# The low half of every fifth weight tile, made by an adding transfer

## The chip, the cores and the metric

The kernel runs on one core of a Trainium2 chip. The metric is device time in microseconds of that core for one execution; before the change the median of three runs is 1138.33 us (1137.66 to 1138.64). PE is the matrix engine, DVE the vector engine, ACT the scalar engine, POOL the general-purpose engine, and SP the engine that issues most transfers.

## The reference

A trunk of two layers works on 512 tokens of width 1024 in float32. Cut to what matters:

```python
for l in range(2):
    mod = silu(c) @ w_ada[l] + b_ada[l]            # shift, scale, gate
    u = rms_norm(x) * (1 + scale) + shift
    z = u @ w_in[l]                                # 18 column groups: q, k, v, gates, indexer, merge gates
    ya = sparse_attention(top 128 keys by the indexer's score)
    yb = sliding_window_attention(window 128, grouped heads, sinks)
    yc = stick_breaking_attention()
    merged = sum(sigmoid(m_b) * ((y_b * silu(gate_b)) @ w_br_b[l]))
    x = x + gate * (merged @ w_out[l])
return rms_norm(x) * final_g
```

Most of the arithmetic is the products with `w_in`, `w_br` and `w_out`, 1024 or 512 deep, over all 512 tokens.

## The kernel before

The matrix engine takes operands in a shortened 32-bit type (fp32r). To keep float32 accuracy, each operand is split into a high half, the operand rounded to that type, and a low half, the operand less its high half. A product then takes three matmuls: high by high, high weight by low activation, low weight by high activation. In the program's names `uh` and `ul` are the halves of the normalised activations, `whi` and `wlo` those of a weight tile.

Weights come in chunks of 128 x 512 (a few of 128 x 384 and 128 x 364). The class `Chunks` (from line 733) holds the sequence of all of them in the order of use, and does three things for chunk number i. `load` issues its transfer from HBM into a `wstage` tile, on SP's queue. `do_split` makes the halves: a cast of `wstage` to `whi`, on ACT, DVE or POOL, and a subtraction `wstage - whi` to `wlo`, on DVE or POOL. `get` hands the two to the matmuls. The split of a chunk stands up to three chunks ahead of its use; `wstage`, `whi` and `wlo` have four buffers each, so a chunk's halves can be written once the chunk four places earlier is used up. Some chunks, those of the conditioning product `w_ada`, are used raw, unsplit, by DVE. They count in the numbering.

A phase with the column groups `FIRST` (chunks of 512 and 384 columns, from `w_first`) opens each layer. The value phase follows (`w_v`, 364 columns a chunk; here the weight streams and the activation stands). Then come many streams woven together: the tiles of `w_t`, three mixers, the branch products (`w_br`), the conditioning product of the next layer. The output product (`w_o`) closes the layer.

The order of the instructions on each engine isn't that of the code. Every operation is recorded (class `Recorder`), with the engines that could do it, and `forward` lays all of them out by list scheduling: at each step the operation that can start first goes to its engine, by the prices in `price` and by priorities that `latest` works out from the round before. `order` does five rounds and keeps the one that ends first in the planner's own reckoning. So the order on every engine depends on what the planner assumes a transfer takes. `emit` then issues everything in that order, which is why nearly all instructions of the profile carry the line of `emit`, 621. In `price` a transfer that POOL issues holds POOL for 1.0; its `lag`, the bytes over a rate, and the lines in `forward` that the diff touches say when its data is there.

`both(out, a, b, op)` records a two-input operation for POOL or DVE. `cast(out, x, scale)` records a copy with rounding: without a scale for ACT, DVE or POOL, with a scale for ACT (`activation` with `Copy`) or DVE (`tensor_scalar`).

Of the kernel before, what the change touches and what calls it, by code (L numbers as in the profile page):

```python
# [29 lines left out]
OP = mybir.AluOpType  # L30
# [251 lines left out]
class Recorder:  # L282
# [149 lines left out]
    def forward(self):  # L432
        E = {e: {"free": 0.0, "port": 0.0, "mode": None, "ready": {}, "pend": []} for e in self.real}
        dma_free, lanes = 0.0, []
# [12 lines left out]
        def offer(x):  # L447
            if x.left == 0 and x.bound == 0:
                for e in x.alts:
                    heapq.heappush(E[e]["pend"], (max(x.est, x.soft.get(e, 0.0)), x.i))  # L450

        def give(c):
            while c.given < len(c.tiles) and c.free:
                t = c.tiles[c.given]
                c.given += 1
                if not t.users:
                    continue
                at, slot = heapq.heappop(c.free)
                t.slot, t.before, c.held[slot] = slot, c.held.get(slot), t
                for x in waiting[id(t)]:  # L460
                    x.est = max(x.est, at)
                    x.bound -= 1
                    offer(x)
# [7 lines left out]
        while len(out) < len(self.list):  # L471
            best = None
            for name, e in E.items():
                free, port, pend, ready = e["free"], e["port"], e["pend"], e["ready"]
                while pend and pend[0][0] <= free + 1e-9:
                    i = heapq.heappop(pend)[1]
                    ready[i] = self.list[i]
                mine = None
                for i in list(ready):
                    x = ready[i]  # L480
                    if x.taken:
                        del ready[i]
                        continue
                    y = x.alts[name]
                    at = max(free, port) if y.port else free
                    if len(x.alts) > 1 and self.elsewhere(x, name, at, E):
                        continue
                    key = (at, x.prio, i)
                    if mine is None or key < mine:
                        mine = key  # L490
                if mine is None or mine[0] > free + 1e-9:
                    while pend and self.list[pend[0][1]].taken:
                        heapq.heappop(pend)
                    if pend:
                        est, i = pend[0]
                        x = self.list[i]
                        at = max(est, port) if x.alts[name].port else est
                        key = (at, x.prio, i)
                        if (mine is None or key < mine) and not (len(x.alts) > 1 and self.elsewhere(x, name, at, E)):
                            mine = key  # L500
                        elif mine is None:
                            mine = None
                if mine is not None:
                    asked = max(free, self.list[mine[2]].est, self.list[mine[2]].soft.get(name, 0.0))
                    if best is None or (mine[0], asked, mine) < best[:3]:
                        best = (mine[0], asked, mine, name)
            assert best is not None, "no instruction may go"
            (at, _, i), name = best[2:]
            e, x = E[name], self.list[i]
            y = x.alts[name]  # L510
            x.taken, x.engine = True, name
            e["ready"].pop(i, None)
            hold = y.cost
            if name == "PE":
                if e["mode"] is not None and y.mode != e["mode"]:
                    hold += self.ENTER[y.mode]
                e["mode"] = y.mode
            x.start, x.hold = at, hold
            e["free"] = at + hold
            if y.port:  # L520
                E["POOL"]["port"] = at + y.lag + self.CROSS if name == "DVE" else at + hold
                E["DVE"]["port"] = at + y.lag - self.TOPORT
            if y.mode == "dma":
                if not x.writes:
                    x.end = at + 2.1
                else:
                    x.end = dma_free = max(at + (2.1 if at < 20.0 else 2.2 if y.lag < 0.22 else 3.0), dma_free) + y.lag * (1.2 if dma_free < 5.5 else 1.0)
                lanes.append(x.end)
                if name == "SP" and len(lanes) >= self.LANES:
                    e["free"] = max(e["free"], lanes[-self.LANES])  # L530
            else:
                x.end = at + y.lag + (hold - y.cost)
            out.append(x)
            for s in x.succs:
                s.est = max(s.est, x.end + self.between(x, s))
                s.left -= 1
                offer(s)
            for s in x.apart:
                for o in s.alts:
                    if o != name:  # L540
                        s.soft[o] = max(s.soft.get(o, 0.0), x.end + self.NEXT)
                s.left -= 1
                offer(s)
            for t in x.tiles:
                t.users -= 1
                t.done = max(t.done, x.end + self.CROSS)
                if t.users == 0:
                    heapq.heappush(t.pool.free, (t.done, t.slot))
                    give(t.pool)
# [99 lines left out]
def trunk(ctx, tc, xT, vecs, w_ss, w_gt, w_first, w_t, w_v, w_br, w_o, rope, consts, out):  # L649
# [8 lines left out]
    PE, ACT, DVE, POOL, SP = (rec.engine(e) for e in ("PE", "ACT", "DVE", "POOL", "SP"))  # L658
# [23 lines left out]
    f = lambda ap: ap.bitcast(F32)  # L682


    def in_psum(*views):
        return any(v.tile.pool.name[:3] == "ps_" for v in views)

    def cast(out, x, scale=None):
        if scale is None:
            ways = {"ACT": ("copy", (out, x), {}), "DVE": ("tensor_copy", (), dict(out=out, in_=x))}  # L690
            if not in_psum(x):
                ways["POOL"] = ("tensor_copy", (), dict(out=out, in_=x))
        else:
            ways = {"ACT": ("activation", (out, x, AF.Copy), dict(scale=scale)), "DVE": ("tensor_scalar", (out, x, scale, None), dict(op0=OP.mult))}
        rec.add(ways)

    def both(out, a, b, op_):
        how = ("tensor_tensor", (), dict(out=out, in0=a, in1=b, op=op_))
        rec.add({"DVE": how} if in_psum(a, b) else {"POOL": how, "DVE": how})
# [28 lines left out]
    class Chunks:  # L728
# [20 lines left out]
        def do_split(self, upto):  # L749
            while self.nsplit < min(upto + 1, len(self.seq)):  # L750
                i = self.nsplit
                if i >= self.nload:
                    break
                if not self.seq[i][1]:
                    t, n = self.raw.pop(i)
                    h = rec.tile("whi", [P, S], F32R)
                    lo = rec.tile("wlo", [P, S], F32R)
                    cast(h[:, :n], t[:, :n])
                    both(lo[:, :n], t[:, :n], f(h[:, :n]), OP.subtract)
                    self.split[i] = (h, lo)  # L760
                    self.used.add(i)
                self.nsplit += 1
# [1053 lines left out]
```

## Time and profile before

| what | value |
|---|---|
| median of three runs | 1138.33 us |
| the profiled execution, its own time | 1136.31 us |
| its span, first to last instruction | 1134.2 us |
| PE busy | 1116.3 us, 98% |
| DVE busy | 900.4 us, 79% |
| ACT busy | 615.8 us, 54% |
| POOL busy | 254.0 us, 22% |
| subtractions to `wlo` | 315 on DVE, 57 on POOL |
| moved by transfers | 159.86 MB, mean 141 GB/s |

The profile is one execution. Its span stands 2.1 us below the execution's own time. A matmul's row is longer than the distance to the next one, since matmuls are pipelined: PE's pace is read from the starts, its starvation from the list of waits.

### The profile page before, as it was taken

The numbers are of one execution on the slowest core, as the hardware profiler recorded it, in microseconds if no ns is written. First come the engines' busy times: TensorE is split into PE (matmuls) and PEld (weight loads), VectorE is DVE, ScalarE is ACT, GpSimd is POOL, SyncE is SP. The second block draws the span as 40 slices with busy tenths as digits, with TensorE's granted clock in tenths as the row PEclk, the third lists the DMA queues.
The fourth block names the chain that finished last, engine by engine and source line by source line (L and its number), as shares of the span: only waits on it lengthen the run. The fifth ranks groups of instructions, "written<-read, shape, count | busy, mean of one in ns | idle before, by whom it ended". The sixth has DMA issues, their size and how long they took to land.

```text
span 1134.2 us, 17655 instructions
## 1 busy us (share of the span) xinstructions
PE 1116.3 (98%) x5579; PEld 926.8 (82%) x5579; DVE 900.4 (79%) x1966; ACT 615.8 (54%) x1298; POOL 254.0 (22%) x340
## 2 busy tenths in 40 slices
PE   8999999999999999999999999999999999999997
PEld 6899877788878787788898988777888878877886
DVE  7865999999989896677475479999998898666544
ACT  6644765863556563444365357757436466444343
POOL 1110344632113220010011004555421222101101
PEclk9999999999999999999999999999999999999999
DMA  9644334354465566455634342253545445524342
GB/s 341 240 123 129 94 94 127 107 146 152 125 170 154 160 199 179 134 151 177 183 111 111 101 137 84 76 157 105 156 131 145 143 140 149 150 83 148 94 130 102
DMA packets 94301, 159.86 MB, mean 141 GB/s; under 512 B 14592, under 2 KB 29184, under 8 KB 94208
## 3 DMA queue, kind: packets, MB, share of 16 engines
q1 hardware_dynamic: 86096, 146.25, 43.7%
q10 hardware_dynamic: 8112, 12.49, 3.9%
q8 instruction: 44, 0.72, 0.3%
q14 instruction: 49, 0.40, 0.1%
HBM read 125.39 MB, written 4.19 MB: 114 GB/s over the span
## 4 chain that ended last, share of the span: by engine, by line
PE 87%; DVE 4%; DMA 3%; POOL 2%; ACT 1%; issue 1%; SPq 1%; DVEq 0%; POOLq 0%; ACTq 0%
PE ps_z L621 68%; PE ps_s L621 15%; PE ps_s L619 3%; SPq L621 1%; PE ps_z L619 1%; DVE X L621 1%; DMA Y<-in_w_ss 1%; DVE wlo L621 1%; POOL wlo L621 1%; DMA m<-zs 1%; DMA U<-X 1%; POOL Q L621 1%; DMA wstage<-in_w_br_c 0%; DVE m L621 0%; DVE t L621 0%
## 5 line engine op out<-in xcount | busy, mean ns | idle before, releaser
L621 PE MATMUL ps_z<-uh,whi 128*128 128x512 f32 (+1 forms) x905 | 353.9, 392 | 2.1 <-ACT KH L621 1.9
L621 PE MATMUL ps_z<-ul,whi 128*128 128x512 f32 (+1 forms) x905 | 351.5, 389 | 0.0
L621 PE MATMUL ps_z<-uh,wlo 128*128 128x512 f32 (+1 forms) x905 | 351.1, 388 | 0.0
L621 DVE TENSOR_TENSOR wlo<-wstage,whi 128x512 fp32r<-128x512 f32 (+2 forms) x315 | 213.4, 680 | 118.5 <-ACT whi L621 99.4
L621 ACT CAST whi<-wstage 128x512 fp32r<-128x512 f32 (+2 forms) x226 | 133.8, 594 | 237.3 <-PE ps_z L621 142.3
L621 PEld LDWEIGHTS ps_z<-uh,whi 128*128 128x128 f32 x905 | 169.8, 188 | 38.4 <-ACT KH L621 2.3
L621 PEld LDWEIGHTS ps_z<-uh,wlo 128*128 128x128 f32 x905 | 169.8, 188 | 34.5 <-issue 0.2
L621 PEld LDWEIGHTS ps_z<-ul,whi 128*128 128x128 f32 x905 | 169.9, 188 | 33.1 <-issue 0.5
L621 POOL CAST whi<-wstage 128x512 fp32r<-128x512 f32 (+2 forms) x109 | 67.5, 619 | 489.2 <-PE ps_z L621 280.5
L621 PE MATMUL ps_z<-Y,whi 128*128 128x512 f32 x384 | 120.2, 391 | 0.2
L621 POOL TENSOR_TENSOR wlo<-wstage,whi 128x512 fp32r<-128x512 f32 (+1 forms) x57 | 73.2, 1286 | 90.8 <-DVE ul L621 56.8
L621 PEld LDWEIGHTS ps_z<-Y,whi 128*128 128x128 f32 x384 | 71.9, 188 | 16.0 <-ACT Y L621 1.1
L621 ACT ACTIVATE e<-e 128x512 f32<-128x512 f32 x96 | 59.6, 631 | 43.2 <-DVE e L621 41.7
L621 ACT ACTIVATE t<-t,nm 128x256 f32<-128x256 f32 (+3 forms) x128 | 65.3, 511 | 32.1 <-DVE nm L621 20.6
L621 PE MATMUL ps_z<-Y,wlo 128*128 128x512 f32 x192 | 74.8, 390 | 0.0
L621 ACT ACTIVATE t<-t 128x512 f32<-128x512 f32 x110 | 61.7, 631 | 7.3 <-POOL t L621 4.1
L621 DVE MAX8 m<-score 128x8 f32<-128x256 f32 (+2 forms) x96 | 53.2, 556 | 1.8
L621 ACT ACTIVATE e<-ps_z 128x512 f32<-128x512 f32 x68 | 40.2, 592 | 25.3 <-DMA V<-X 13.2
L621 DVE MATCH_REPLACE8 score<-m,score 128x256 f32<-128x256 f32 (+2 forms) x96 | 52.1, 543 | 0.0
L621 DVE STREAM_TRANSPOSE X<-X 128x640 f32<-128x640 f32 (+1 forms) x72 | 49.5, 729 | 1.7 <-ACT X L621 1.5
L621 PE MATMUL ps_s<-KH,Q 128*128 128x256 f32 (+3 forms) x280 | 48.5, 304 | 1.4 <-ACT KH L621 1.4
L621 DVE SCALAR_TENSOR_TENSOR wstage<-wstage,csr 128x512 f32<-128x512 f32 x64 | 45.0, 704 | 5.2 <-DMA wstage<-in_w_ss 5.1
(211 smaller groups left out, 1946.6 us busy)
## 6 DMA issues: line engine op xcount, KB each, us to landing
wstage<-in_w_t SPq DMA_DIRECT2D x212, 256.0 KB, 2.7
wstage<-in_w_v SPq DMA_DIRECT2D x48, 182.0 KB, 2.3
m<-zs SPq DMA_DIRECT2D x128, 64.0 KB, 2.2
wstage<-in_w_gt SPq DMA_DIRECT2D x32, 256.0 KB, 2.7
wstage<-in_w_ss SPq DMA_DIRECT2D x32, 256.0 KB, 2.9
wstage<-in_w_o SPq DMA_DIRECT2D x32, 256.0 KB, 2.7
Y<-in_w_ss SPq DMA_DIRECT2D x15, 512.0 KB, 6.2
wstage<-in_w_first SPq DMA_DIRECT2D x16, 256.0 KB, 4.0
```

The costliest lines, as they stand in the source:

```text
L619: self.real[engine].matmul(*[real(a) for a in q[:3]], start=q[3], stop=True, skip_group_check=True)
L621: made = getattr(self.real[engine], y.op)(*[real(a) for a in y.args], **{k: real(v) for k, v in y.kw.items()})
```

## The change

Where i % 5 is 1, `do_split` no longer subtracts. It writes the negated, rounded weights into `wlo` (`cast` with the scale -1, on ACT or DVE), and then has POOL issue a transfer that reads the same weights from HBM again and adds them onto that tile in SBUF, so that `wlo` ends as the weights less their rounded value. Of the 372 split chunks 69 are made so: 56 of 512 columns, 10 of 364 and 3 of 384. The cast to `whi` stays. Secondly the planner's assumption on transfers is another: up to 20 us it is as it was, up to 60 us every transfer has 3.0 and its lag, and later there are three classes by size with a start-up and a rate each.

```diff
@@ forward
                 if not x.writes:
                     x.end = at + 2.1
                 else:
-                    x.end = dma_free = max(at + (2.1 if at < 20.0 else 2.2 if y.lag < 0.22 else 3.0), dma_free) + y.lag * (1.2 if dma_free < 5.5 else 1.0)
+                    late, rate = (2.1, 1.2 if dma_free < 5.5 else 1.0) if at < 20.0 else (3.0, 1.0) if at < 60.0 else (2.3, 1.57) if y.lag > 0.4 else (2.0, 1.78) if y.lag > 0.19 else (2.2, 0.0)
+                    x.end = dma_free = max(at + late, dma_free) + y.lag * rate
@@ do_split
                     cast(h[:, :n], t[:, :n])
-                    both(lo[:, :n], t[:, :n], f(h[:, :n]), OP.subtract)
+                    if i % 5 == 1:
+                        cast(lo[:, :n], t[:, :n], -1.0)
+                        POOL.dma_start(lo[:, :n], self.seq[i][0], accum_op=OP.add)
+                    else:
+                        both(lo[:, :n], t[:, :n], f(h[:, :n]), OP.subtract)
```

Since the planner works anew from both edits, the order moves on every engine. Of the negated casts 53 stand on ACT and 16 on DVE; DVE keeps 247 subtractions and POOL 56. In the places below a name's number counts the program's tiles, `whi_197` being one buffer of `whi`; the numbers differ a little between the two programs.

The first place is PE's queue in the opening phase, where chunk 1 (the 384 columns) is the first with an adding transfer. Before, its low half is `wlo_203`:

```order
L621 MATMUL ps_s_238<-uh0_222,wlo_208 128x256
L621 MATMUL ps_s_240<-uh0_222,wlo_203 128x256
L621 MATMUL ps_s_242<-uh0_222,wlo_203 128x256
L621 MATMUL ps_z_244<-uh0_222,wlo_203 128x256
L621 MATMUL ps_s_242<-uh0_222,whi_197 128x256
```

After, it is `wlo_200`:

```order
L622 MATMUL ps_z_231<-uh1_282,whi_237 128x512
L622 MATMUL ps_z_233<-uh1_282,whi_237 128x512
L622 MATMUL ps_s_235<-uh1_282,whi_237 128x512
L622 MATMUL ps_s_241<-uh0_221,wlo_200 128x256
L622 MATMUL ps_s_243<-uh0_221,wlo_200 128x256
L622 MATMUL ps_z_245<-uh0_221,wlo_200 128x256
```

Its first use moved from the 24th of the phase's matmuls to the 40th, behind three matmuls of the next slice of the activations.

The second place is POOL's queue in the value phase of the first layer. Before:

```order
L621 CAST whi_628<-wstage_568 128x364
L621 CAST whi_651<-wstage_579 128x364
L621 CAST whi_702<-wstage_596 128x364
L621 CAST KH_755<-zc_646 128x512
L621 CAST Q_792<-zc_672 64x512
L621 CAST Q_843<-zc_795 64x512
L621 CAST whi_849<-wstage_785 128x364
```

After:

```order
L622 DMA wlo_594<-in_w_v 128x364
L622 CAST whi_632<-wstage_564 128x364
L622 CAST whi_655<-wstage_584 128x364
L622 CAST whi_706<-wstage_599 128x364
L622 DMA wlo_725<-in_w_v 128x364
L622 TENSOR_TENSOR zc_676<-zc_676,m2_702 128x512
L622 CAST Q_802<-zc_676 64x512
L622 CAST Q_855<-zc_784 64x512
L622 DMA wlo_848<-in_w_v 128x364
L622 CAST whi_877<-wstage_807 128x364
```

Adding transfers (the rows with DMA) now stand between POOL's casts of other chunks, five in this phase of each layer.

The third place is POOL's queue later in the first layer, where key, query and mixer work meets the splits (`m2` and `zc` are rotary terms, `Q` a query's halves, the MEMSETs of `t` and the copy to `Y` belong to the stick-breaking mixer). Before:

```order
L621 TENSOR_TENSOR m2_2213<-m2_2213,rt_84 128x512
L621 MEMSET t_2268 128x1
L621 TENSOR_TENSOR wlo_2322<-wstage_2207,whi_2303 128x512
L621 CAST whi_2334<-wstage_2243 128x512
L621 MEMSET t_2274 128x1
L621 CAST Y_2343<-e_2271 128x512
L621 MEMSET t_2288 128x1
L621 TENSOR_TENSOR zc_2211<-zc_2211,m2_2213 128x512
L621 TENSOR_TENSOR wlo_2363<-wstage_2243,whi_2334 128x512
L621 CAST Q_2365<-zc_2211 64x512
L621 TENSOR_TENSOR Q_2365<-zc_2211,Q_2365 64x512 x2
L621 MEMSET t_2300 128x1
```

After:

```order
L622 TENSOR_TENSOR zc_2217<-zc_2217,m2_2228 128x512
L622 CAST whi_2306<-wstage_2270 128x512
L622 CAST Q_2313<-zc_2217 64x512
L622 TENSOR_TENSOR wlo_2322<-wstage_2270,whi_2306 128x512
L622 CAST whi_2334<-wstage_2273 128x512
L622 MEMSET t_2290 128x1
L622 CAST Q_2313<-zc_2217 64x512
L622 MEMSET t_2299 128x1
L622 TENSOR_TENSOR wlo_2350<-wstage_2273,whi_2334 128x512
L622 TENSOR_TENSOR Q_2313<-zc_2217,Q_2313 64x512
L622 MEMSET t_2320 128x1
L622 TENSOR_TENSOR Q_2313<-zc_2217,Q_2313 64x512
```

Two subtractions to `wlo` stay on POOL ahead of the last MEMSETs; the product to `m2` has left it, and so the two-input operations of the piece go from six to five.

## The prediction

> **What bounds the kernel now.** I read the page's busy times and chain first, then windows of the span, then the list of what PE waited for.
>
> ```profile
> span 1134.2 us, 17655 instructions
> ...
> PE 1116.3 (98%) x5579; PEld 926.8 (82%) x5579; DVE 900.4 (79%) x1966; ACT 615.8 (54%) x1298; POOL 254.0 (22%) x340
> ...
> PE 87%; DVE 4%; DMA 3%; POOL 2%; ACT 1%; issue 1%; SPq 1%; DVEq 0%; POOLq 0%; ACTq 0%
> ```
>
> PE is the bound: 98% busy, 87% of the chain that ended last. No edit here touches its work, so only its idle time can shrink. The windows (after the bounds: length, busy us and instructions of PE, PEld, DVE, ACT, POOL, granted clock, transfers' share, GB/s) show where that lies:
>
> ```profile
> 0.00:30.00 30.00, 25.41 (x123) 19.81 (x124) 24.17 (x51) 19.66 (x38) 3.30 (x9) 1.00 0.95 339
> ...
> 200.00:300.00 100.00, 99.03 (x490) 80.52 (x489) 98.68 (x251) 57.40 (x134) 41.48 (x48) 1.00 0.42 124
> 300.00:400.00 100.00, 96.62 (x472) 78.02 (x471) 88.38 (x223) 58.14 (x140) 20.60 (x21) 1.00 0.59 167
> ...
> 500.00:600.00 100.00, 100.00 (x527) 86.40 (x526) 61.61 (x118) 44.95 (x78) 6.92 (x8) 1.00 0.51 152
> ...
> 700.00:800.00 100.00, 98.60 (x500) 77.83 (x497) 96.52 (x220) 66.53 (x139) 49.80 (x70) 1.00 0.42 117
> ```
>
> Between the opening and the end PE idles only in three of them, 0.97 + 3.38 + 1.40 = 5.75 us, and there DVE is busy 88 to 99%. The list of PE's waits (total us, times, longest) puts names to it:
>
> ```profile
> PE ps_s L621 <- ACT t L621: 2.1, 2, 1.2
> PE ps_s L621 <- DVE V L621: 1.9, 1, 1.9
> PE ps_z L621 <- ACT KH L621: 1.9, 1, 1.9
> PE ps_s L621 <- DVE t L621: 1.4, 2, 1.0
> PE ps_s L621 <- ACT KH L621: 1.4, 1, 1.4
> PE ps_s L621 <- DVE epst L621: 1.0, 1, 1.0
> PE ps_s L621 <- ACT e L621: 0.6, 1, 0.6
> PE ps_s L621 <- DMA wstage<-in_w_first: 0.2, 1, 0.2
> ```
>
> The two on `ACT t` (0.9 and 1.2) and the two on `ACT KH` are those of the middle, together 5.4 us; the others belong to the opening and the end. No row names `whi` or `wlo`: PE never waits for a split weight. So the ceiling of a gain is 5.4 us, and a loss has no such ceiling, since a late `wlo` would stop PE where today nothing does.
>
> **The change part by part.** First the work that moves off DVE:
>
> ```profile
> L621 DVE TENSOR_TENSOR wlo<-wstage,whi 128x512 fp32r<-128x512 f32 (+2 forms) x315 | 213.4, 680 | 118.5 <-ACT whi L621 99.4
> ...
> L621 DVE TENSOR_SCALAR e<-e 128x512 f32<-128x512 f32 x70 | 30.6, 438 | 2.7 <-ACT e L621 2.6
> ...
> L621 ACT CAST whi<-wstage 128x512 fp32r<-128x512 f32 (+2 forms) x226 | 133.8, 594 | 237.3 <-PE ps_z L621 142.3
> ...
> L621 POOL CAST whi<-wstage 128x512 fp32r<-128x512 f32 (+2 forms) x109 | 67.5, 619 | 489.2 <-PE ps_z L621 280.5
> ...
> L621 POOL TENSOR_TENSOR wlo<-wstage,whi 128x512 fp32r<-128x512 f32 (+1 forms) x57 | 73.2, 1286 | 90.8 <-DVE ul L621 56.8
> ```
>
> DVE loses 68 subtractions, 68 x 0.680 = 46.2 us, and gains 16 negated casts at the row of a one-input operation, 16 x 0.438 = 7.0: 39 us less of 900. ACT gains 53 x 0.594 = 31.5 us and comes to 57%, with 237 us of idle time ahead of its casts alone; I cost that at nothing. Without this cover each cast would delay ACT by 0.6 us. POOL gains 69 issues. How long one holds POOL no row shows: at least as long as its shortest instruction, 0.1 us, at most its two-input operation, 1.29; I take 1.0, the middle of the two rows above that work on whole tiles, since for 128 rows something has to be written each time. That is 69 us on top of 254, and 31% busy.
>
> Then the path of one `wlo`. The pace of a chunk is read from PE's starts, twelve matmuls apart, in the value phase and in the stage of the `w_t` tiles (start us, length, row):
>
> ```profile
> 73.93 0.33 PE L621 MATMUL ps_z<-whi,uh 128*128 128x364 f32 x1
> ...
> 75.93 0.33 PE L621 MATMUL ps_z<-whi,uh 128*128 128x364 f32 x1
> ...
> 199.75 0.39 PE L621 MATMUL ps_z<-uh,whi 128*128 128x512 f32 x1
> ...
> 202.49 0.39 PE L621 MATMUL ps_z<-uh,whi 128*128 128x512 f32 x1
> ```
>
> With four buffers a `wlo` can be written from the end of the chunk four places earlier, and is needed three chunks later: 3 x 2.00 = 6.0 us in the value phase, 3 x 2.74 = 8.2 us among the tiles. What goes into that is the negated cast (0.50 and 0.62, in proportion to the row's 0.594), the issue, and the landing, for which the nearest rows are plain transfers (count, KB each, median us from issue to landing):
>
> ```profile
> wstage<-in_w_t SPq DMA_DIRECT2D x212, 256.0 KB, 2.7
> wstage<-in_w_v SPq DMA_DIRECT2D x48, 182.0 KB, 2.3
> ...
> Y<-in_w_ss SPq DMA_DIRECT2D x15, 512.0 KB, 6.2
> ```
>
> The adding transfer reads its destination too. From the first two rows a KB costs 0.4 us / 74 = 5.4 ns, so as much data again adds 1.0 and 1.4 us: I take landings of 3.3 and 4.1 us, between the plain rows (2.3 and 2.7) and the row of twice the size (6.2). The sum is 0.50 + 1.0 + 3.3 = 4.8 us against 6.0, and 0.62 + 1.0 + 4.1 = 5.7 against 8.2. Spare: 1.2 and 2.5 us. So I cost the new path at nothing; the window of three chunks hides it. At the upper bounds, 0.50 + 1.29 + 6.2 = 8.0 and 0.62 + 1.29 + 6.2 = 8.1, the tiles just hold and the value phase is 2.0 us late.
>
> Next the traffic: 56 x 256 + 10 x 182 + 3 x 192 KB = 16.7 MB more.
>
> ```profile
> q1 hardware_dynamic: 86096, 146.25, 43.7%
> ```
>
> 146.25 MB take 43.7% of the transfer engines, so this adds 5 points, or 10 if counted twice: hidden, but for the opening, where the share is 0.95. Two of the transfers stand there (192 and 256 KB), at 339 GB/s 0.58 + 0.77 = 1.35 us. The order lets PE use the first of them only sixteen matmuls later than before, so I take 0 and keep 1.35 as the upper bound; below nothing is excluded, for nothing moves out of the opening's transfers.
>
> Last the new order. Whichever way the planner's new assumption moves things, the bounds are the four waits: all gone, -5.4, or as much again, +5.4. What I expect of them goes by where they come from. POOL's rows ahead of the first `ACT t` wait:
>
> ```profile
> 204.23 1.29 POOL L621 TENSOR_TENSOR m<-m,rt 128x512 f32<-128x512 f32 x1
> ...
> 205.52 1.29 POOL L621 TENSOR_TENSOR wlo<-wstage,whi 128x512 fp32r<-128x512 f32 x1
> ...
> 209.21 1.29 POOL L621 TENSOR_TENSOR wlo<-wstage,whi 128x512 fp32r<-128x512 f32 x1
> ...
> 211.25 2.65 POOL L621 TENSOR_TENSOR Q<-zc,Q 64x512 fp32r<-64x512 f32 x2
> 213.84 0.13 POOL L621 MEMSET t<- 128x1 f32 x2
> ```
>
> POOL runs without a pause up to the MEMSETs that release ACT's `t`. The new order has one two-input operation less there, 1.29 us, more than the 0.9 that PE waited: I take all 0.9. Layer 2 has its like near 769 us; there I take half of the 1.2. The two waits on `ACT KH` hang on rotary copies:
>
> ```profile
> 327.62 2.04 DMA m<-zs
> ...
> 374.24 3.36 DMA m<-zs
> ```
>
> No relief shortens those; but DVE subtractions stand in the same stretches (88% busy), and one of 0.68 taken out ahead of each wait gives 0.7 each. Together 0.9 + 0.6 + 0.7 + 0.7 = 2.9 us.
>
> Sum: the profiled execution took 1136.31 us, 2.0 below the median of the runs. 1136.31 - 2.9 = 1133.4 for such an execution, and with the 2.0 again **1135.4 us**, 0.26% faster.
>
> **The rivals.** *No change.* The four waits are chains of latency, and a new order opens others of the same size. For it speaks that all four end on ACT, which gets more work; against it that DVE is nearly full just there. Time: 1138.3, give or take 2.
>
> *POOL's issues run late: slower.* Two rows by tile show what DVE and POOL do to each other today (ns, least, median, most):
>
> ```profile
> L621 DVE TENSOR_TENSOR wlo<-wstage,whi x315: 523/682/1567, 14.5 to 1114.5; 128x512 fp32r<-128x512 f32 x129, 128x364 fp32r<-128x364 f32 x24, 128x384 fp32r<-128x384 f32 x5
> ...
> L621 POOL CAST whi<-wstage x109: 486/615/1114, 38.2 to 1083.8; 128x512 fp32r<-128x512 f32 x98, 128x364 fp32r<-128x364 f32 x10, 128x384 fp32r<-128x384 f32 x1
> ```
>
> The same operation can take 0.5 to 0.9 us more when the other engine is in the way. If every issue is held up so, each `wlo` still has its spare, but POOL's own work behind it (casts, `Q`, `zc`) is late. Some twelve issues stand where POOL is busy 40 to 50% and on the chain: 12 x 0.9 = 10.8 us, and with three quarters of it reaching PE 8.1: 1138.3 + 8.1 = 1146.4. It decides from an issue of about 1.9 us. Against it: elsewhere POOL is idle four fifths of the time. [...]
>
> *The landing is long: slower.* If adding costs what the 512 KB row shows, 6.2 us, the value phase is late by 0.50 + 1.0 + 6.2 - 6.0 = 1.7 us at each of its ten adding transfers, 17 us: 1155. It decides from a landing of 4.5 us. For it: the value phase has the smallest spare and PE is full there. Against it: that row comes from the crowded opening.
>
> **How the numbers follow.** About 0.2%, 2.3 us, is what a measurement can tell from no change. Forecast 0.50 (of it 0.08 inside the 0.2%), no change 0.20, POOL's issues 0.20, the landing 0.10. Hence faster 0.42, same 0.28, slower 0.30. The forecast's own range is 1133 (all 5.4 gone) to 1137.5. The range to hold 8 in 10 runs from 1132.5, the ceiling of the gain with the runs' half us, to 1148, past the POOL case; beyond it lies the landing.
>
> **What would show it.** Right: no wait of PE on `wlo` or on an adding transfer; landings under 4.5 us; DVE near 861 us and ACT near 647 us busy; PE's idle time in 200 to 400 and 700 to 800 us down from 5.75 to about 3 us; POOL's gap around an issue about 1 us. Wrong: rows of PE waiting for `wlo` in the value phases (60 to 110 and 615 to 665 us); POOL gaps near 2 us with later `Q` and `zc`; PE idle as before, with other names.

## The result: 1% slower, and the profile after

The changed kernel takes 1150.64 us (median of 4 runs, 1146.91 to 1153.38) against 1138.2 us for the kernel before beside it: a ratio of 1.0107, 95% interval 1.0072 to 1.0142. It is slower by about 12 us, where 1135.4 was forecast, and the time lies above the range of 1132.5 to 1148. The profiled execution is the slowest of the four, 1153.38 us. All comparisons below are ratios to the kernel before, run beside it on the same chip; 0.1% is 1.14 us.

The page of the changed kernel, span, busy times and the chain that ended last:

```profile
span 1151.6 us, 17827 instructions
...
PE 1122.2 (97%) x5579; PEld 927.8 (81%) x5579; DVE 875.2 (76%) x1923; ACT 631.1 (55%) x1335; POOL 316.2 (27%) x415
...
PE 56%; DMA 6%; DVE 5%; ACT 2%; issue 2%; SPq 1%; POOL 1%; ACTq 0%; DVEq 0%; POOLq 0%
```

DVE has lost 25 us and ACT gained 15, yet PE's share of the chain fell from 87% to 56% and the transfers' doubled. The same windows as before the change (bounds, then length, busy us and instructions of PE, PEld, DVE, ACT, POOL, granted clock, transfers' share, GB/s):

```profile
0.00:30.00 30.00, 24.81 (x124) 19.49 (x125) 23.10 (x49) 19.05 (x38) 3.56 (x10) 1.00 0.97 349
200.00:300.00 100.00, 98.87 (x495) 80.19 (x496) 95.70 (x248) 56.71 (x130) 46.18 (x53) 1.00 0.53 144
300.00:400.00 100.00, 92.06 (x436) 73.67 (x436) 79.69 (x197) 53.86 (x134) 27.12 (x30) 0.97 0.63 166
500.00:600.00 100.00, 99.08 (x521) 85.39 (x520) 65.27 (x130) 47.39 (x84) 14.16 (x17) 1.00 0.64 179
700.00:800.00 100.00, 98.48 (x507) 77.11 (x506) 95.89 (x193) 68.78 (x132) 57.31 (x83) 1.00 0.43 111
```

The window from 300 to 400 us stands out: 92.06 us of PE where there were 96.62, and a granted clock below 1.00, which no window of before showed ahead of the end. What PE waited for (total us, times, longest):

```profile
PE ps_s L622 <- ACT KH L622: 5.1, 1, 5.1
PE ps_z L620 <- DMA U<-X: 3.5, 2, 2.7
PE ps_s L622 <- DVE t L622: 2.4, 3, 1.1
...
PE ps_z L622 <- DMA wlo<-in_w_t: 1.3, 2, 0.8
...
PE ps_z L622 <- DMA wlo<-in_w_first: 0.9, 1, 0.9
...
PE ps_z L622 <- DMA wlo<-in_w_br_b: 0.6, 1, 0.6
...
PE ps_s L622 <- DMA wlo<-in_w_v: 0.3, 1, 0.3
```

The four rows on `wlo` are new, 3.1 us in all. The two large rows name something else: `KH`, a copy of a key's halves on ACT, and `U<-X`, a small transfer from one place of SBUF to another. The transfers themselves, queues first (packets, MB, share of 16 engines), then issues (count, KB each, median us to landing):

```profile
q1 hardware_dynamic: 86288, 146.48, 43.1%
q0 software_dynamic: 9936, 17.14, 9.7%
...
wlo<-in_w_t POOLq DMA_DIRECT2D x39, 256.0 KB, 4.7
...
Y<-in_w_ss SPq DMA_DIRECT2D x15, 512.0 KB, 7.8
wstage<-in_w_first SPq DMA_DIRECT2D x16, 256.0 KB, 5.6
...
wlo<-in_w_v POOLq DMA_DIRECT2D x10, 182.0 KB, 3.9
```

q0 holds the adding transfers: 0.57% of the engines for each MB, against 0.29% on q1. Loads of other streams take longer than before the change: `Y<-in_w_ss` 7.8 us after 6.2, `wstage<-in_w_first` 5.6 after 4.0.

### The profile page after: what moved, and what is told of

The parts are those of the page before. It is cut to its first block, busy times and chain, and to the rows that moved or that the text cites. A ratio compares the mean times of both kernels' runs of the same rounds, so it can differ in the third digit from the quotient of the medians.

```text
span 1151.6 us, 17827 instructions
## 1 busy us (share of the span) xinstructions
PE 1122.2 (97%) x5579; PEld 927.8 (81%) x5579; DVE 875.2 (76%) x1923; ACT 631.1 (55%) x1335; POOL 316.2 (27%) x415
## 3 DMA queue, kind: packets, MB, share of 16 engines
q0 software_dynamic: 9936, 17.14, 9.7%
## 4 chain that ended last, share of the span: by engine, by line
PE 56%; DMA 6%; DVE 5%; ACT 2%; issue 2%; SPq 1%; POOL 1%; ACTq 0%; DVEq 0%; POOLq 0%
PE ps_z L622 45%; PE ps_s L622 8%; PE ps_s L620 3%; DMA m<-zs 1%; DMA V<-X 1%; ACT t L622 1%; SPq L622 1%; PE ps_z L620 1%; DMA wlo<-in_w_t 1%; DVE X L622 1%; DVE wlo L622 1%; DMA wlo<-in_w_first 1%; DMA wstage<-in_w_ss 0%; DVE zc L622 0%; DVE e L622 0%
## 5 line engine op out<-in xcount | busy, mean ns | idle before, releaser
L622 DVE TENSOR_TENSOR wlo<-wstage,whi 128x512 fp32r<-128x512 f32 (+2 forms) x247 | 168.1, 683 | 116.0 <-ACT whi L622 97.5
L622 ACT CAST whi<-wstage 128x512 fp32r<-128x512 f32 (+2 forms) x221 | 130.9, 594 | 228.6 <-PE ps_z L622 148.5
L622 POOL CAST whi<-wstage 128x512 fp32r<-128x512 f32 (+1 forms) x112 | 68.8, 615 | 320.1 <-PE ps_z L622 156.6
L622 DVE MAX8 m<-score 128x8 f32<-128x384 f32 (+2 forms) x96 | 53.3, 556 | 1.8
L622 POOL DMA_DIRECT2D wlo<-in_w_t x39 | 34.2, 876 | 71.9 <-ACT wlo L622 33.5
L622 PEld LDWEIGHTS ps_s<-KH,Q 128*128 128x128 f32 x280 | 42.9, 191 | 12.5 <-ACT KH L622 5.6
```

The lines of the kernel that those rows point to most:

```text
L622: made = getattr(self.real[engine], y.op)(*[real(a) for a in y.args], **{k: real(v) for k, v in y.kw.items()})
```

## The experiments

Both kernels issue the same 5579 matmuls, and in the runs that keep the changed kernel's order they stand in the same order too. For these runs the start of each matmul can be set beside its start in another run, and the places where the distance grows are the places of the loss. "By place" below means that.

**One edit at a time.** *e1_plan_only* has the planner's new assumption alone, *e2_adds_only* the adding transfers alone.

```diff
 e1_plan_only: the change's lines in forward, and in do_split as before:
+                    both(lo[:, :n], t[:, :n], f(h[:, :n]), OP.subtract)
 e2_adds_only: the change's lines in do_split, and in forward as before:
+                    x.end = dma_free = max(at + (2.1 if at < 20.0 else 2.2 if y.lag < 0.22 else 3.0), dma_free) + y.lag * (1.2 if dma_free < 5.5 else 1.0)
```

> Edit: the planner's new assumption on transfers alone; every low half is subtracted as before, no adding transfer. Theory A (the adding transfers cost the time, by their landing and by what they do to other transfers): no change, 1136 to 1140 us. Theory B (the new assumption gives a worse order): slower, 1145 to 1152 us, with the long wait of PE for a key near 335 us again.

> Edit: the adding transfers with the planner's old assumption. Theory A: 1146 to 1153 us, as the change. Theory B: back near 1138 us. If both edits only shake the order (theory C, a new order is luck), anything between 1136 and 1155 with waits at other places.

Measured: 1141.77 us, ratio 1.0036 (1.0024 to 1.0048), and 1162.25 us, 1.0217 (1.0200 to 1.0234). Neither edit gains anything, and the adding transfers alone are worse than both together. The first lies between the ranges of its theories, the second above all of its own.

**The order and DVE's relief without the bytes.** *e3_tiny* issues every adding transfer, at its place, with 8 columns, and so leaves out the rest of those low halves.

```diff
+                if "accum_op" in y.kw:
+                    self.real[engine].dma_start(real(y.args[0])[:, :8], y.args[1][:, :8], **y.kw)
+                    continue
```

> Edit: the changed kernel's order, instruction for instruction, but each adding transfer moves only 8 columns of its chunk (the other columns keep the negated rounded weights, so the low halves are left out there). Theory A: the traffic is gone and a landing falls to about 2 to 2.5 us; PE's waits on low halves vanish, the long waits near 335 and 384 us shrink, 1136 to 1141 us. Theories B and C: the order is the same, so 1146 to 1152 us.

Measured: 1132.47 us, ratio 0.9951 (0.9936 to 0.9966). Its page, windows and first waits:

```profile
PE 1115.1 (99%) x5579; PEld 925.8 (82%) x5579; DVE 873.5 (77%) x1923; ACT 632.8 (56%) x1335; POOL 317.6 (28%) x415
```

```profile
200.00:300.00 100.00, 100.00 (x497) 81.89 (x497) 97.61 (x260) 62.21 (x149) 45.12 (x52) 1.00 0.47 130
300.00:400.00 100.00, 100.00 (x487) 81.05 (x486) 88.47 (x217) 55.99 (x132) 32.31 (x34) 1.00 0.61 172
```

```profile
PE ps_s L625 <- DVE t L625: 2.2, 3, 1.0
PE ps_s L625 <- ACT t L625: 1.6, 3, 0.8
PE ps_s L625 <- DVE V L625: 1.5, 1, 1.5
```

With the bytes gone, the kernel is 0.5% faster than before, and faster than any of the theories had it. PE is busy without a break from 200 to 400 us, and the waits on `KH` and `U<-X` have gone. The bytes cost 1.56% of the time, 17.8 us.

**Which property of the transfers costs it.** *e4_plain* copies the same bytes through the same queue without adding. *e5_scratch* adds, with 352 columns, onto a tile that nobody reads, after the negated cast, so that PE never waits for a landing.

```diff
 e4_plain
+                    self.real[engine].dma_start(real(y.args[0]), y.args[1])
 e5_scratch
+                    made = self.real[engine].dma_start(self.scratch[0][:, :min(w, 352)], y.args[1][:, :min(w, 352)], **y.kw)
```

> Edit: the changed kernel's order, but the 69 transfers are plain ones of the same size from POOL (the low half is overwritten by the weights: the subtraction is left out). This takes the adding alone away. Theory A with the adding at fault: a packet of 2048 B takes about 84 ns in place of 178, a landing about 3.5 us in place of 4.7, 1138 to 1143 us. Theory A with mere traffic at fault, and theories B and C: 1146 to 1152 us.

> Edit: the changed kernel's order; each adding transfer waits for its negated cast as before, but adds onto a scratch tile that nothing reads (352 of 512 columns, as much as fits), so no matmul waits for its landing; the low halves keep the negated rounded weights, the remainder being left out. The traffic stays at 71% of the bytes, the waits on low halves go. Theory A1 (the adding packets slow the other transfers, which are on the path of keys and mixers): most of the 18 us between the small transfers (1132.5) and the change (1150.6) stays, 1142 to 1149 us. Theory A2 (the low halves' own landing is what PE waits for, directly or through buffers freed late): 1131 to 1136 us.

Measured: 1140.65 us, ratio 1.0024 (1.0006 to 1.0042), and 1139.97 us, 1.0018 (1.0004 to 1.0031). In e4_plain the queue's row, the landing of the large ones, and the time that one issue holds POOL (ns, least, median, most):

```profile
q0 software_dynamic: 9936, 17.14, 5.4%
...
wlo<-in_w_t POOLq DMA_DIRECT2D x39, 256.0 KB, 3.4
```

```profile
L623 POOL DMA_DIRECT2D wlo<-in_w_t x39: 530/576/745, 113.1 to 1051.6; - x39
```

The same row of the changed kernel:

```profile
L622 POOL DMA_DIRECT2D wlo<-in_w_t x39: 827/875/936, 114.9 to 1066.4; - x39
```

So adding, compared with copying the same bytes, holds the transfer engines 1.8 times as long (9.7% against 5.4%), lands 1.3 us later and holds POOL 0.3 us longer. In time, the plain copies cost 8.3 us over e3_tiny, and making them additions costs 9.4 more (differences of the ratios, uncertain by 2.7 and 4.5). e4_plain came out where its theory of the adding had it, yet nearly half of the loss is there without the adding. In e5_scratch, with 12.44 MB in place of 17.14, 7.6 us are lost, between the ranges of its two theories, although PE waits for none of the landings: traffic alone, through other streams' copies. PE's two stops on `KH` and `U<-X` are there too, shorter:

```profile
PE ps_s L629 <- ACT KH L629: 2.3, 1, 2.3
...
PE ps_z L620 <- DMA U<-X: 1.9, 1, 1.9
```

How long a transfer takes beside an adding one can be read pair by pair, since the runs of this order issue the same 912 other transfers in the same order. The 250 that the changed kernel issues while an adding transfer is under way take 1.1 us longer, at the median, than the same ones in e3_tiny; for the other 662 the median difference is 0.0. In e5_scratch the figure is 0.7 us for 212, and beside the plain copies of e4_plain 0.4 for 182.

**A planner that knows.** *e6_honest* tells the planner that an adding transfer takes 3.0 and 2.6 times its lag. *e7_calm* does so too, and has only 18 of them, all in the stretch of the stick-breaking mixer.

```diff
+                    if "accum_op" in y.kw:
+                        late, rate = 3.0, 2.6
 e7_calm also
+                    if i % 3 == 1 and self.seq[i][2] == 1:
```

> Edit: the change, with the planner told what an adding transfer took: 3.0 and 2.6 times its lag (4.8 for 256 KB) and that it holds the transfer engines as long. Theory A1: the order can keep low halves from being late but not the traffic off the others, 1143 to 1152 us. Theory A2: the order makes room for the landings, 1132 to 1138 us.

> Edit: as the run with the planner told, but adding transfers only in the part of each layer where the stick-breaking mixer runs, every third chunk there: 17 transfers in place of 69, where DVE is fullest and the transfer engines are at about 0.4. Theory A1: a quarter of the traffic where it meets little, 1134 to 1140 us, at best a little faster than before. Theory A2 says the same or better; theory C (a new order is luck) 1134 to 1146.

Measured: 1148.71 us, ratio 1.0096 (1.0075 to 1.0117), with PE waiting 5.3 us for `wlo<-in_w_t`, and 1142.23 us, 1.0045 (1.0032 to 1.0057). So telling the planner the price didn't mend it here; as each of these is another order, that doesn't exclude a part of the planner's.

**Is e3_tiny's gain that of any such order?** *e8_tiny_other* takes the chunks with i % 5 equal to 3, with 8 columns.

> Edit: as the run with transfers of 8 columns, but for the chunks with i % 5 equal to 3 in place of 1, so that the planner makes another order with the same relief of DVE. If the relief of DVE is worth the 5.6 us that the small transfers gained: 1131 to 1135 us. If that gain was the luck of one order: anything between 1132 and 1143, with 1138 to 1142 as likely as below.

Measured: 1148.70 us, ratio 1.0098 (1.0074 to 1.0122). With much the same relief of DVE (875.3 us busy) and next to no bytes, another order loses 1% where e3_tiny gained 0.5%; neither theory had it so slow. The distance between the two orders, 1.5%, is more than the whole change's 1.1%.

**Where the bytes hurt.** By place, the changed kernel loses 21.0 us on e3_tiny in the profiled executions, and 11.2 of them between 322 and 396 us (in e3_tiny's time): two stops of PE, 5.15 and 2.69 us, and behind each 3.41 us at half the clock, 1.7 us more. The 17th to the 23rd adding transfer are issued around there. *e9_tiny_mid* cuts these seven to 8 columns, *e10_full_mid* cuts all the others.

```diff
+                    self.nadd = getattr(self, "nadd", -1) + 1
 e9_tiny_mid:  8 columns where
+                    if 16 <= self.nadd <= 22:
 e10_full_mid: 8 columns where
+                    if not 16 <= self.nadd <= 22:
```

> The changed kernel's order, with seven of its 69 adding transfers (the 17th to the 23rd, which were issued between 295 and 381 us) cut down to 8 columns; the low halves of those seven tiles are left as negated weights. Theory (the loss sits in that stretch, where the added bytes delay copies that PE waits for through `KH` and `U`, and half-clock pieces follow): 11 us of the loss go, 1139 to 1141 us, and the stretch from 300 to 400 us is full of PE's work again. Rival (the loss is spread over all adding transfers, each a little late): 7/69 of 18 us go, 1148 to 1150.

> The converse: only the 17th to the 23rd adding transfer are full, the other 62 move 8 columns (their tiles' low halves are left as negated weights). Theory (that stretch carries the loss): 1132.5 of the run with small transfers only, plus 10 to 11, 1142 to 1144 us, with waits on `KH` and `U<-X` and the half-clock pieces after them. Rival (spread): 1132.5 + 2, 1134 to 1135, no half-clock piece in the middle of the span.

Measured: 1143.77 us, ratio 1.0064 (1.0049 to 1.0079), and 1137.43 us, 1.0004 (0.9984 to 1.0024; the runs lie wide, 1134.99 to 1144.49). Both theories miss. By either run the seven cost 0.43 to 0.53% (5 to 6 us, about 0.8 each) and the other 62 together 1.03 to 1.13% (12 to 13 us, 0.2 each); each of these differences is uncertain by 2 to 5 us. The stretch is the worst, but it carries a third and not the bulk. By place, e9_tiny_mid is only 1.8 us behind e3_tiny there.

What happens in that stretch can be read in the changed kernel. The chain of waits from 317 us (start, length, what) and POOL's issues:

```profile
317.10 5.45 DMA wstage<-in_w_ss
...
333.75 2.34 DMA m<-zs
...
339.42 0.63 ACT KH L622
```

```profile
317.07 0.85 POOL L622 DMA_DIRECT2D wlo<-in_w_t  x1
...
334.40 0.86 POOL L622 DMA_DIRECT2D wlo<-in_w_t  x1 [0.58 <-DVE wlo L622]
```

The load of `in_w_ss` leaves in the same instant as an adding transfer and takes 5.45 us, where 3.0 is the median of its kind in this run and the same load took 3.63 in e3_tiny; DVE's work on it, the rotary copies and then `KH` all come later. PE stops for 5 us, and then starts again at half its pace:

```profile
334.55 0.40 PE L622 MATMUL ps_z<-uh,wlo 128*128 128x512 f32 x1
340.09 1.75 PE L622 MATMUL ps_s<-KH,Q 128*128 128x512 f32 x4 [5.15 <-ACT KH L622]
341.64 0.63 PE L622 MATMUL ps_z<-uh,whi 128*128 128x512 f32 x1
342.07 0.63 PE L622 MATMUL ps_z<-ul,whi 128*128 128x512 f32 x1
...
343.52 0.40 PE L622 MATMUL ps_z<-uh,wlo 128*128 128x512 f32 x1
343.76 0.40 PE L622 MATMUL ps_z<-uh,whi 128*128 128x512 f32 x1
```

Matmuls start 0.43 us apart, and later 0.24. The second stop is a copy of the same kind: an adding transfer leaves at 380.52, and in the chain a `U<-X`, 2.9 to 3.1 us at the median and 3.57 for the same one in e3_tiny, takes 4.67:

```profile
380.88 4.67 DMA U<-X
385.54 0.97 issue
386.52 3.53 PE ps_z L620 x16
```

The late load isn't the whole of the first stop. Set beside e3_tiny instruction by instruction, at 314 us PE ran 4.0 us late but DVE already 6.7; behind the load DVE was 10.1 us late, and at 335 us PE ran into that. So about half of the stop had gathered on DVE before this load. In e10_full_mid, where only the seven transfers are full, DVE is never more than 1.5 us late on e3_tiny from 255 to 340 us, and PE doesn't stop at that place. This explains why neither theory held. The traced execution is the slowest of the four, so the length of its two stops is its own. That the adding transfers delay these copies is inferred from the pairs above and from e3_tiny, where the stops are gone; the trace doesn't show one packet waiting for another.

**Other ways to take the subtraction from DVE, or none.** *e11_pool_sub* keeps the order and lets POOL subtract, with no negated cast and no adding transfer. *e12_dve_sub* does the same with the subtraction on DVE, at the place where the later of the two casts stood in the changed order. *e13_mixed* is e12_dve_sub with 40 adding transfers kept.

```diff
 e11_pool_sub; e12_dve_sub has "DVE" for "POOL"
+                if q and len(q[3]) == 2:
+                    q[3].add("done")
+                    made = self.real["POOL"].tensor_tensor(out=real(q[0]), in0=real(q[1]), in1=real(q[2]), op=OP.subtract)
 e13_mixed: subtracted on DVE where
+                        if self.nadd < 3 or 16 <= self.nadd < 30 or self.nadd == 35 or 55 <= self.nadd < 66:
```

> The changed kernel's order without negated casts and without adding transfers: POOL subtracts the rounded half instead, at the place behind the rounding (69 subtractions, 1.29 us each for a 512-column tile, on top of POOL's 254 us of before). No traffic is added and DVE keeps its relief of 68 subtractions. Theory (the order is good and the traffic alone spoils it): 1132 to 1136 us, faster than the kernel before. Rival (POOL's 1.29 us per tile come where POOL's `Q`, `zc` and `KH` are on the path, or slow DVE beside them): 1140 or more, with PE waits on POOL's names.

> The changed kernel's order, but every adding transfer and its negated cast is replaced by the subtraction of before, on DVE at that place: no added traffic, none of the 69 issues on POOL, and DVE has its 46 us back. Theory A (the 0.5% gained by the small transfers came from the order): 1132 to 1135 us, faster than before. Theory B (it came from DVE's relief; without it the same order is a worse one): 1139 to 1145, with PE waits on DVE's names and on what DVE feeds.

> The same, but with 40 of the 69 adding transfers kept: those of the stretches from 45 to 260, 530 to 570 and 585 to 905 us and behind 1070 us, where the traces showed next to no loss beside them; the other 29 are subtractions on DVE. If the loss of an adding transfer depends on its place alone: what e12_dve_sub gives, less up to 3 us for DVE's relief, plus 1 to 2 for landings, so no slower than e12_dve_sub by more than 1 us. If every added transfer costs its 0.2 us wherever it stands: 8 us more than e12_dve_sub.

Measured: 1146.05 us, ratio 1.0080 (1.0065 to 1.0095); 1147.41 us, 1.0088 (1.0072 to 1.0104); 1141.82 us, 1.0047 (1.0033 to 1.0062).

e12_dve_sub shows where the 0.5% of e3_tiny came from. The same order with DVE's subtractions put back is 1.37% (15.6 us) slower than e3_tiny, and slower than before, whose order was planned with them; it is slower than theory B had it, and theory A falls. Its timeline shows one place, DVE first and then PE:

```profile
213.51 2.32 DVE L630 TENSOR_TENSOR_SCAN t<-ps_s,t 128x511 f32<-128x511 f32 x2
215.97 1.76 DVE L640 TENSOR_TENSOR wlo<-wstage,whi 128x512 fp32r<-128x512 f32 x1
217.66 0.68 DVE L630 SCALAR_TENSOR_TENSOR t<-ps_s,t 128x512 f32<-128x512 f32 x1
218.25 0.68 DVE L630 TENSOR_TENSOR zc<-ps_z,rt 128x512 f32<-128x512 f32 x1
```

```profile
218.99 0.63 PE L630 MATMUL ps_z<-Y,whi 128*128 128x512 f32 x1 [1.81 <-DVE zc L630]
```

The returned subtraction (1.76 us here in place of 0.68) makes `zc` late, and PE waits 1.81 us for it.

In e11_pool_sub the subtractions leave DVE, but DVE's other work slows down. Here is one two-input group of it, 729 ns a piece in e3_tiny, and POOL's added subtractions (ns, least, median, most):

```profile
L630 DVE TENSOR_TENSOR xm<-xm,sm 128x512 f32<-128x512 f32 x32 | 28.3, 883 | 0.3
```

```profile
L640 POOL TENSOR_TENSOR wlo<-wstage,whi x69: 967/1292/2055, 14.3 to 1113.9; 128x512 fp32r<-128x512 f32 x56, 128x364 fp32r<-128x364 f32 x10, 128x384 fp32r<-128x384 f32 x3
```

DVE is busy 890.6 us where e3_tiny has 873.5 with 16 instructions more. So the relief is partly taken back, and 1132 to 1136 was wrong; the rival's "1140 or more" held, with 2.0 us of PE's waits on POOL's `KH`.

e13_mixed is 0.41% (4.7 us) faster than e12_dve_sub, as the theory of place allowed and the other didn't. By place it loses 0.5 us on e3_tiny between 42 and 285 us, and nothing between 578 and 861, with full adding transfers in both. There the added bytes cost next to nothing, so their cost goes more by place than by the piece. They aren't free there every time: with the same transfers the changed kernel's trace loses 2.6 us between 42 and 285. Where its 29 subtractions are back on DVE, e13_mixed loses 2.4 us in the opening, most of it beside a piece at half clock after 2.04 us of idle time, and 3.7 from 322 to 396 us. No version here beats the kernel before; the only faster one, e3_tiny, leaves work out.

## Why the prediction was wrong, point by point

| from before to after | run | ratio | step |
|---|---|---|---|
| the new order, DVE still subtracting | e12_dve_sub | 1.0088 | +0.88% |
| DVE relieved; casts and issues added | e3_tiny | 0.9951 | -1.37% |
| the bytes, as plain copies | e4_plain | 1.0024 | +0.73% |
| the bytes, added | after | 1.0107 | +0.83% |

**What bounds the kernel, and the ceiling.** Right in the main. With all but the bytes of the change the gain is 0.49%, 5.6 us (uncertain by 1.7), and the ceiling had been put at 5.4 from four waits of PE. (A fourth window idles too, 0.20 us from 120 to 200, which the prediction passed over.) Those from 200 to 400 us are gone in e3_tiny. That the two figures agree so well is partly luck: from 700 to 800 us PE idles 1.56 us there, where it had 1.40, and the two profiled executions differ by 4.0 us.

**The new order, -2.9 us.** As an account of the change without its bytes, the sign was right and the size half of what it became. But its working, one instruction fewer ahead of each wait, treated order and relief as a few small shifts. They are +10 and -15.6 us, in this order, and e8_tiny_other shows that a neighbouring order turns the sum to +11. So the right sign was luck.

**DVE -39, ACT +31.5, POOL.** The edit's own terms held: DVE's subtractions to `wlo` fell by 45.3 us (213.4 to 168.1) and 16 negated casts took 6.8. DVE came to 875.2 and not 861 because the planner gave it other work, and ACT to 631.1 and not 647 for the converse. POOL's issue took 0.88 us where 1.0 was taken. POOL's share was summed wrongly, though without effect: 254 and 69 us make 28% of the span and not 31%; 27% were measured.

**The landing, and "the window of three chunks hides it".** The landing was well sized: 4.7 us from the start of the issue, where 1.0 + 4.1 had been taken, and 3.9 where 1.0 + 3.3 had. So was the window, from the end of the buffer's last use to the first use of the new `wlo`: counted along PE's order, with four uses of each `wlo`, it is 8.0 us or more among the tiles and 6.17 at the median in the value phase, against 8.2 and 6.0. The step failed at the places where the cast or the issue didn't start when the buffer came free. One of them, POOL's queue:

```profile
424.27 0.61 POOL L622 CAST Q<-zc 64x512 fp32r<-64x512 f32 x1 [8.89 <-DVE klow L622]
424.94 0.61 POOL L622 CAST KH<-KH 64x512 fp32r<-64x512 f32 x1
425.50 0.88 POOL L622 DMA_DIRECT2D wlo<-in_w_t  x1
```

and PE:

```profile
430.31 0.50 PE L622 MATMUL ps_z<-uh,wlo 128*128 128x512 f32 x1 [0.76 <-DMA wlo<-in_w_t]
```

The cast had started 1.9 us after the buffer came free, and its issue left 3.3 us after the cast's end, behind two casts that waited for `klow`. Of the 10.7 us of that window 4.8 were left for a landing. Such queues were not in the path as it was summed. The price is 3.1 us in PE's waits on `wlo`, and 5.4 at most by place.

**"Next the traffic ... hidden".** This is the step that failed: it put the cost of the added bytes at nothing, and they cost 17.8 us. The share was bounded rightly (5 or 10 points; 9.7 measured, for 17.14 MB), but a share isn't what the traffic costs. It makes single copies late that PE waits for (a load of 5.45 us, a `U<-X` of 4.67), in stretches where these have no spare, and it does so without PE ever waiting for an adding transfer: 7.6 us in e5_scratch. The prediction looked for loss only on `wlo` itself. In the opening 0 was taken, with 1.35 us as upper bound; by place the changed kernel has lost 2.2 us on e3_tiny by 105 us.

**The rivals.** *No change* came nearer than the forecast, but no case held the cause. *POOL's issues run late* didn't happen: all 39 issues of `in_w_t` lie between 827 and 936 ns, with DVE 76% busy, where the case needed 1.9 us. What DVE and POOL do to each other's operations stands in the trace of before: the 230 subtractions of 512 columns on DVE that had no operation of POOL beside them took 646 to 694 ns, and each of the longer ones, up to 1567, had one. Nor did the adding transfers leave much later behind their issues than plain ones. Behind the opening, the changed kernel's first packets left 1.5 to 3.0 us after the start of the issue, at the median 1.85, against 1.7 for the plain copies of e4_plain. The longest landing took 7.1 us, at 200 us, and its first packet left after 2.5. *The landing is long* forecast 1155, near the time, by another road: it had the value phase late by 17 us, and PE waited there for 0.3.

**The signs named beforehand.** "No wait of PE on `wlo`" failed, by 3.1 us; "landings under 4.5 us" failed by a little if read as the row gives it; "PE's idle time down to about 3 us" failed, at 10.6 us in the three windows. The sign that mattered, rows on `KH` and `U<-X` with longer copies, was not on the list.

## What to carry to other kernels

A transfer that takes work off a busy engine is not priced by the share of the transfer engines that it fills (9.7% here, for bytes that cost 17.8 us), but by the copies on the critical chain that move beside it: look for the stretches where the matrix engine waits for small copies, and keep added bytes out of them. An operation's window must be counted from when its first step really starts in its engine's queue, not from when its buffer comes free. Where a planner lays out the order, compare an edit with itself less its payload in the same order, as e3_tiny does, before a gain or a loss is put down to the edit.

## What the runs showed of the hardware

An adding transfer of 256 KB landed after 4.7 us, a plain one through the same queue after 3.4, and one through SP's queue after 2.8; one of 8 columns, 4 KB, still took 3.0 (all are medians). The adding transfers held the transfer engines 1.8 times as long as plain copies of the same bytes, and the issue of one held POOL for 0.88 us in place of 0.58. With 8 columns the issue was no shorter, 0.88 us in e3_tiny, and the packets no fewer, 9936 for the 69. In the changed kernel a packet of 2048 B took 178 ns at the median on q0, and 84 on q1.

Two stops of PE cost 1.7 us more each than their length. After the 5.15 us of idle time at 335 us, and the 2.69 at 384, the granted clock was 0.5 for 3.41 us each:

```profile
340.00:345.00 5.00, 4.91 (x16) 4.08 (x17) 4.44 (x10) 0.66 (x2) 1.01 (x2) 0.68 0.71 178
...
387.00:392.00 5.00, 5.00 (x23) 3.20 (x20) 4.22 (x9) 2.25 (x4) 2.99 (x4) 0.66 0.32 116
```

The idle time ahead of such a piece has no sharp limit here: 1.81 us in e12_dve_sub at 217 us were followed by one, and 1.88 us in the kernel before at 378 us were not. In the fifteen traces of this case no idle time of PE under 1.66 us was followed by such a piece, and every one from 2.64 us up was; between the two it went either way. The prediction's upper bound of the new order left this out.
